# A hybrid decoder block on one core: first attention values from x, and fifteen value products in a new order

## The chip, the cores and the metric

The kernel runs on one core of one Trainium2 chip. Its time is the device time of one execution in microseconds (us); three runs of the kernel before gave 2204.49, 2204.80 and 2205.09 us.

## The reference, cut to what matters

One sequence of 1024 tokens with 1024 channels passes a block of retention and dilated attention, and then an MLP. Only its head matters here:

```python
mod = silu(c) @ w_ada + b_ada            # shift, scale, ... of 1024 channels each
h = rms_norm(x, norm1_g) * (1 + scale) + shift
proj = h @ w_in                          # rq, rk, rv (2048 wide), rg, three groups of aq, ak, av (512 wide each), gates
```

With r(t) the reciprocal root mean square of token t, and a1 = norm1_g (1 + scale), the row of h for token t is r(t) a1 x(t) + shift. So for a weight W, h W = r(t) (a1 x(t)) W + shift W, in which the second part is one row for all tokens.

## The kernel before, in words

Everything is float32. TensorE multiplies in a rounded form (fp32r); each float32 factor is split into a rounded part (`hh`, "hi") and a remainder (`hl`, "lo"), and a product is three matmuls: hi by lo, lo by hi, hi by hi (`mm3`, L203 to L211). ScalarE (ACT) writes the rounded part, VectorE (DVE) the remainder. A matmul of these stages has 128 rows, 128 stationary columns and 512 moving columns.

All instructions stand in an order written out by hand; each engine runs its own in that order, and the DMAs that SP issues are in one order too, which stops where a DMA has to wait for its buffer. Buffers come from pools: `x4` tiles (26 of 512 KB), `wraw` (3, raw weights), `whl` (3 each for `wh` and `wl`). TensorE's results lie in eight banks of PSUM.

The stages, and what they run:

- **Start** (`startup`, L401 to L442). SP loads c, all of x by rows of tokens (`xn`, 8 tiles of 512 KB), the constants, and then for each of 8 row blocks k of 128 channels two rows of the modulation weights (`em`, scale and shift) and the channel-major block of x (`xt`, 512 KB each). ACT squares each `xn` (L428) for the mean square, POOL takes the power (L380), and two sets of four small matmuls (`rstd_bcast`, L387) spread r(t) over the partitions. DVE makes each modulation value by a product with silu(c), 128x1024, with its sum (`mod1`, L463).
- **First attention values** (`av_first`, `av_k`, L796 to L849). For each k, DVE scales `xt` by a1 and r(t) (`h1_scale`, L486), ACT adds the shift and rounds (L488), DVE takes the remainder (L491), and TensorE adds 24 matmuls onto eight banks, one for each block of 128 tokens (L811): group 0.
- **Other attention values** (`av_step`): the same with 192 matmuls each for groups 1 and 2. Beside them, DVE and ACT make sums of blocks of h (`sums_of_h`, t1, t2, t3; L884 to L902; t4 comes in the next stage).
- **Queries, keys, gates** (`queries_keys`, L1007): 18 pairs, each a 2 by 2 block product by seven products of 12 matmuls (Winograd's form: 11, s1, s3, s2, 12, 22, s4 use blocks of h or their sums, and blocks of the weight or their sums). Beside them DRAM to DRAM copies and additions prepare weight sums for later (`copy_block`, `quarter_sums`; the additions are POOL's DMAs that accumulate, L564).
- **Retention values** (`values`, L1117): two halves of seven products of 48 matmuls each, with weights from those sums; `v_post` (L1087) puts the results together, and writes them to `v_d` in DRAM.
- Then retention itself, attention, and the MLP, which the change doesn't touch.

## Time and profile before

| | |
|---|---|
| median of three runs | 2204.8 us |
| profiled execution, first to last instruction (span) | 2203.6 us |
| what the median has beyond that span | 1.2 us |
| TensorE (PE) busy | 2170.7 us, 99% |
| VectorE (DVE), ScalarE (ACT), GpSimd (POOL) busy | 1456.9, 922.9, 160.6 us |

The profile is of one execution, whose time beyond its span isn't listed. A row of a timeline has the start, the duration, the engine, the line, and what is written from what; in brackets stands the idle time before it and what ended that. Matmuls overlap: one takes 0.39 us in a row, while the next begins 0.23 us after it.

### The profile page before, as it was taken

To read this page: it belongs to the slowest core of one execution; us is meant where nothing else is said; L and a number is where in the kernel's file an instruction comes from. 1 tells how busy PE (TensorE), PEld (TensorE's weight loads), DVE (VectorE), ACT (ScalarE), POOL (GpSimd) and SP (SyncE) were. 2 spreads that over 40 slices of the span, in tenths; PEclk is the share of its full clock that TensorE was granted. 3 is DMA by queue.
4 is the path that set the end of the run, shared out by engine and by line. 5 is a ranking of instruction groups with operands and counts; after the bars stand their busy time and mean duration, and the time that the engine had idled before them with its cause. 6 is when DMAs were issued, how large, how long until landed. Compare 5 with 4: busy or idle time off the path is not lost. (4 is left out here: it accounts for less than half of the span.)

```text
span 2203.6 us, 27246 instructions
## 1 busy us (share of the span) xinstructions
PE 2170.7 (99%) x10134; PEld 1802.4 (82%) x10134; DVE 1456.9 (66%) x2284; ACT 922.9 (42%) x1691; POOL 160.6 (7%) x192
## 2 busy tenths in 40 slices
PE   7999999999999999999999999999999999999998
PEld 4888888888887888888888888888778888888887
DVE  6618777763547778865564754677876665887855
ACT  4323332223334445444554634524455445533413
POOL 0001111000011122111100000001100000000003
PEclk9999999999999999999999999999999999999999
DMA  9539999634676556557863265654144344745322
GB/s 367 202 128 284 304 289 292 193 115 172 233 267 209 166 179 220 177 161 197 195 173 97 87 244 186 239 179 160 62 166 152 146 149 177 262 136 175 119 86 77
DMA packets 156611, 408.93 MB, mean 186 GB/s; under 512 B 27446, under 2 KB 55357, under 8 KB 153278
## 3 DMA queue, kind: packets, MB, share of 16 engines
q1 hardware_dynamic: 148542, 363.14, 46.8%
q0 software_dynamic: 7936, 44.05, 9.2%
q8 instruction: 80, 1.31, 0.2%
q14 instruction: 53, 0.43, 0.1%
HBM read 316.27 MB, written 156.13 MB: 214 GB/s over the span
## 5 line engine op out<-in xcount | busy, mean ns | idle before, releaser
L207 PE MATMUL qap<-hh,qaw 128*128 128x512 f32 x216 | 84.0, 389 | 0.0
L209 PE MATMUL qap<-hl,qaw 128*128 128x512 f32 x216 | 84.0, 389 | 0.0
L211 PE MATMUL qap<-hh,qaw 128*128 128x512 f32 x216 | 84.0, 389 | 0.0
L638 POOL TENSOR_TENSOR j<-qk,j 128x512 fp32r<-128x512 f32 x32 | 43.3, 1353 | 458.3 <-ACT j L637 441.7
L1902 POOL TENSOR_TENSOR accnf<-accnf,sqnf 128x256 f32<-128x256 f32 (+1 forms) x18 | 16.6, 922 | 609.6 <-ACT sqnf L1898 609.6
L2006 ACT ACTIVATE a<-a 128x512 f32<-128x512 f32 x48 | 30.3, 631 | 73.3 <-DVE a L2005 73.3
L1322 ACT ACTIVATE P<-P,ng 128x128 f32<-128x128 f32 (+1 forms) x96 | 42.0, 439 | 37.5 <-DVE ng L1319 37.5
L264 DVE TENSOR_TENSOR qaw<-wa,qaw 128x512 fp32r<-128x512 f32 x54 | 36.0, 685 | 30.4 <-ACT qaw L254 30.4
L2214 ACT CAST w2h<-w2s 128x512 fp32r<-128x512 f32 x36 | 22.4, 622 | 80.0 <-DVE w2s L2252 78.8
L264 DVE TENSOR_TENSOR fw<-w1r,fw 128x512 fp32r<-128x512 f32 x48 | 32.9, 688 | 33.6 <-ACT fw L254 33.6
L207 PE MATMUL fp<-h2h,fw 128*128 128x512 f32 x128 | 50.0, 391 | 0.0
L211 PE MATMUL fp<-h2h,fw 128*128 128x512 f32 x128 | 49.8, 389 | 0.0
L209 PE MATMUL fp<-h2l,fw 128*128 128x512 f32 x128 | 49.8, 389 | 0.0
L207 PE MATMUL roa<-rh,rwl 128*128 128x512 f32 x128 | 49.8, 389 | 0.0
L209 PE MATMUL roa<-rl,rwh 128*128 128x512 f32 x128 | 49.8, 389 | 0.0
L211 PE MATMUL roa<-rh,rwh 128*128 128x512 f32 x128 | 49.8, 389 | 0.0
L1737 DVE TENSOR_TENSOR rwl<-rwl,rwh 128x1024 fp32r<-128x1024 f32 x25 | 30.2, 1221 | 29.0 <-ACT rwh L1767 29.0
L673 ACT COPY sm<-sT 128x128 f32<-128x128 f32 x32 | 8.5, 267 | 93.8 <-PE sT L661 93.8
L207 PEld LDWEIGHTS qap<-hh,qaw 128*128 128x128 f32 x216 | 40.6, 188 | 8.5
L211 PEld LDWEIGHTS qap<-hh,qaw 128*128 128x128 f32 x216 | 40.6, 188 | 8.4
L209 PEld LDWEIGHTS qap<-hl,qaw 128*128 128x128 f32 x216 | 40.6, 188 | 8.4
L1902 POOL TENSOR_TENSOR accn<-accn,sqn 128x512 f32<-128x512 f32 x12 | 15.5, 1293 | 392.2 <-ACT sqn L1898 392.2
(3104 smaller groups left out, 7211.6 us busy)
## 6 DMA issues: line engine op xcount, KB each, us to landing
v<-vd SPq DMA_DIRECT2D x32, 512.0 KB, 5.0
raw<-in_w_ada_dram SPq DMA_DIRECT2D x32, 512.0 KB, 5.0
w1r<-in_w_ff_dram SPq DMA_DIRECT2D x32, 512.0 KB, 4.8
vd<-vo SPq DMA_DIRECT2D x24, 512.0 KB, 6.4
yt<-y POOLq DMA_DIRECT2D x24, 512.0 KB, 6.9
xsd<-as SPq DMA_DIRECT2D x24, 512.0 KB, 2.7
w2r<-in_w_ff2s_dram SPq DMA_DIRECT2D x24, 512.0 KB, 7.2
em<-in_w_ada_dram SPq DMA_DIRECT2D x16, 512.0 KB, 10.2
```

The costliest lines, as they stand in the source:

```text
L207: nc.tensor.matmul(o, wl, xh, start=first, stop=False, skip_group_check=skip)
L209: nc.tensor.matmul(o, wh, xl, start=False, stop=False, skip_group_check=skip)
L211: nc.tensor.matmul(o, wh, xh, start=False, stop=last, skip_group_check=skip)
L264: nc.vector.tensor_sub(t[:, 512:], src, fv(t[:, :512]))
L638: nc.gpsimd.tensor_sub(t[:, 1], src, fv(t[:, 0]))
L673: nc.scalar.copy(sm, ps[:, :C])
L1322: nc.scalar.activation(v, v, AF.Exp, bias=ng[:, blk:blk + 1], accum_out=st[:, g, blk, 2 + a:3 + a])
L1737: nc.vector.tensor_sub(lo, fv(lo), fv(hi))
L1902: (nc.vector if f == 7 else nc.gpsimd).tensor_add(G["acc", key], G["acc", key], sq)
L2006: nc.scalar.activation(o, o, AF.Relu)
L2214: nc.scalar.copy(hi, src)
```

## The change

The first attention values (group 0) are made from a1 x without r(t) and without the shift: `plain_split`, `plain_low`; the result is multiplied by r(t) when it leaves PSUM. The shift's row is made beside the later products: DVE multiplies the raw weight's rows by the shift and adds them up in the tile `decay` (`shift_rows`), one float32 matmul with ones adds over the partitions, and four accumulating DMAs add it to the values in DRAM (`shift_out`). So x by rows, r(t), and the modulation's shifts are loaded after the first blocks of weights, and c is loaded straight to 128 partitions. The bias table's and constants' loads are issued from ACT's queue.

Then `more_values` runs eleven products of 48 matmuls. The first four are the retention values' products 11 and 12 of both halves, whose blocks of h and of the weight are not sums (`r0`, `r1`). Block 11 is finished there; the bare product 11 is kept in DRAM (`m11_d`), and `values` copies it back into PSUM (`v_base`). The other seven (`av`) give the attention values of groups 1 and 2 as one 1024 wide product in Winograd's form; its weight sums are made by POOL's accumulating DMAs into SBUF (`u_add`). `values` then has five products for each half in place of seven, and the copies of the weights for the moved ones go. The rows of h are made in halves between these products (`h_scale`, `h_split`), and so are the sums t1 to t4; the last remainder is always queued behind the next step (`late_low`). `a_load(1, ...)`, the table `decay` and cosines are loaded at other places, as the code shows.

```diff
-        xn = [x4(f"xn{b}") for b in range(NC)]
-        for b in range(NC):
-            nc.sync.dma_start(xn[b], io["x"][b])
...
-        for b in range(NC):
-            nc.scalar.activation(xn[b], xn[b], AF.Square, accum_out=ss1[:, b:b + 1])
-        for g in range(3):
-            bias_rows(g)
-        rs = rstd_of(ss1, "n1", xpool)
-        mod1(0)
...
+    def late_low(f=None):
+        if first["lows"]:
+            first["lows"].pop()()
+        if f:
+            first["lows"].append(f)
+    def plain_split(k, ts):
+        nc.scalar.mul(hh[k][:, ts], xt[k][:, ts], a1[:, k:k + 1])
+    def plain_low(k):
+        nc.vector.scalar_tensor_tensor(hl[k], xt[k], a1[:, k:k + 1], fv(hh[k]), op0=ALU.mult, op1=ALU.subtract)
+    def scale_mod(k):
+        mod1(k, (SC1,))
+        nc.vector.scalar_tensor_tensor(a1[:, k:k + 1], mods[:, SC1 + k:SC1 + k + 1], bs1[:, k:k + 1],
+                                       vec[:, VC_N1 + k:VC_N1 + k + 1], op0=ALU.add, op1=ALU.mult)
+    def shift_mod(k):
+        mod1(k, (SH1,))
+        sh = mods[:, SH1 + k:SH1 + k + 1]
+        nc.vector.tensor_add(sh, sh, vec[:, VC_BADA + SH1 + k:VC_BADA + SH1 + k + 1])
+    def h_scale(k, j):
+        t = xt[k][:, 512 * j:512 * j + 512]
+        nc.vector.scalar_tensor_tensor(t, t, a1[:, k:k + 1], rb1[0][:, 512 * j:512 * j + 512],
+                                       op0=ALU.mult, op1=ALU.mult)
+    def h_split(k, j):
+        ts, sh = slice(512 * j, 512 * j + 512), mods[:, SH1 + k:SH1 + k + 1]
+        t, hi, lo = xt[k][:, ts], hh[k][:, ts], hl[k][:, ts]
+        nc.scalar.activation(hi, t, AF.Identity, bias=sh)
+        late_low(lambda: nc.vector.scalar_tensor_tensor(lo, t, sh, fv(hi), op0=ALU.add, op1=ALU.subtract))
...
+              if src != "w_rv" or n not in ("11", "12")]
...
+    def first_values(ahead):
+        H0, H1 = slice(0, 512), slice(512, 1024)
+        nc.sync.dma_start(vec, io["vec"])
+        nc.sync.dma_start(cb, io["c"].to_broadcast([P, D]))
+        nc.scalar.dma_start(rel[:32], io["rel_bias"])
+        for g in range(3):
+            nc.scalar.dma_start(bias_cut(onehot, g)[:33], io["onehot"][:, 384 * g:384 * g + 384])
+        nc.scalar.dma_start(ct, io["cst"])
+        nc.vector.memset(rel[32:33], 1.0)
+        loads = []
+        for k in range(NK):
+            loads += [(xn_load, b) for b in {3: (0, 1, 2), 4: (3, 4), 5: (5,), 6: (6, 7)}.get(k, ())]
+            loads += [(ada_load, SC1 + k), (x_load, k)]
+            if k == 0:
+                loads.append((wa_load, 0, (H0, H1)))
+            if k in (2, 4, 6):
+                loads.append((wa_load, k // 2))
+        loads += [(ada_load, SH1 + k) for k in (0, 2, 4, 6)] + [(u_load, 0)]
+        loads += [(ada_load, SH1 + k) for k in (1, 3, 5, 7)] + [(u_load, 1)]
+        def more(n):
+            for f, *args in [loads.pop(0) for _ in loads[:n]]:
+                f(*args)
+        more(17)
+        nc.scalar.activation(cb, cb, AF.Silu)
+        nc.vector.tensor_scalar_add(bs1, vec[:, VC_BADA + SC1:VC_BADA + SC1 + NK], 1.0)
+        for g in range(3):
+            bias_rows(g)
+        scale_mod(0)
+        wa_split(0, (H0,))
+        plain_split(0, H0)
+        plain_split(0, H1)
+        wa_split(0, (H1,))
+        wh, wl = (fv(t) for t in wa[0][1:])
+        plain_low(0)
+        nc.vector.tensor_sub(wa[0][2][:, H0], wa[0][0][:, H0], wh[:, H0])
+        av = [ps_s(f"av{c}") for c in range(NC)]
+        def mms(k, parts, cs_=range(NC)):
+            w, ws = wa[k // 2][1:], slice((k % 2) * 512, (k % 2) * 512 + 512)
+            for c in cs_:
+                for x, j in parts:
+                    nc.tensor.matmul(av[c], x[k][:, c * C:(c + 1) * C], w[j][:, ws], start=k == 0 and (x, j) == (hh, 0),
+                                     stop=k == NK - 1 and (x, j) == (hl, 0), skip_group_check=True)
+        squares = {2: (0, 1, 2), 3: (3, 4), 4: (5,), 5: (6, 7)}
+        for k in range(NK):
+            more((2, 3, 4, 5, 6, 9, 2, 0)[k])
+            for b in squares.get(k, ()):
+                xn_square(b)
+            if k + 1 < NK:
+                scale_mod(k + 1)
+                for ts in (H0, H1):
+                    plain_split(k + 1, ts)
+                if k % 2 == 1:
+                    wa_split((k + 1) // 2)
+                plain_low(k + 1)
+                if k == 0:
+                    nc.vector.tensor_sub(wa[0][2][:, H1], wa[0][0][:, H1], wh[:, H1])
+                if k % 2 == 1:
+                    raw, hi, lo = wa[(k + 1) // 2]
+                    nc.vector.tensor_sub(lo, raw, fv(hi))
+            if k == 5:
+                rs = rstd_of(ss1, "n1", xpool)
+                rb1.append(x4("rb1"))
+            if k == 0:
+                mms(k, [(hh, 0)])
+                mms(k, [(hl, 0)])
+                mms(k, [(hh, 1)])
+            elif k < NK - 1:
+                mms(k, [(hh, 1), (hh, 0)])
+                mms(k, [(hl, 0)])
+        for m in range(4):
+            shift_mod(2 * m)
+        u_w(0, 0)
+        u_w(0, 1)
+        late_low()
+        for c in range(NC):
+            mms(NK - 1, [(hh, 1), (hh, 0), (hl, 0)], [c])
+            if c % 2 == 0:
+                t = x4(f"avo{c}")
+            o = t[:, DV * (c % 2):DV * (c % 2) + DV]
+            nc.scalar.mul(o, av[c], rs[:, c:c + 1])
+            nc.sync.dma_start(va_d[0][c * C:(c + 1) * C], o)
+            if c in (3, 5):
+                j = (c - 3) // 2
+                nc.scalar.copy(rb1[0][:, 512 * j:512 * j + 512], rstd_bcast(rs, 4 * j, 4, f"n1{j}"))
+            if c == 3:
+                h_scale(0, 0)
+                h_split(0, 0)
+        for m in range(1, 4):
+            h_scale(2 * m, 0)
+            h_split(2 * m, 0)
+        late_low()
+    UPLAN = {"11": ("11", 1, "a"), "12": ("21", 1, "b"), "s1": ("t1", 1, "c"), "s2": ("t2", -1, "a"),
+             "s4": ("22", 1, "c"), "s3": ("t3", -1, "a"), "22": ("t4", -1, "a")}
+    USEQ = [("r0", "11"), ("r1", "11"), ("r0", "12"), ("r1", "12")] + [("av", n) for n in UPLAN]
+    U = {}
+    m11_d = [dram.tile([P, 4, 512], F32, name=f"m11d{hp}") for hp in range(2)]
...
+    def u_load(i):
+        n = USEQ[i][1]
+        for j in range(2):
+            if i in (1, 7):
+                t = x4(f"ur{i}{j}")
+            elif i in (3, 5, 9):
+                t = whl.tile([P, 1024], F32, tag=("wh", "wl")[j], name=f"ur{i}{j}")
+            else:
+                t = wraw.tile([P, 1024], F32, tag="raw", name=f"ur{i}{j}")
+            U["raw", i, j] = t
+            nc.sync.dma_start(t, u_block(i, "21" if n[0] == "s" else n, j))
+    def u_add(i):
+        n = USEQ[i][1]
+        for blk in {"s1": ("22",), "s2": ("22", "11"), "s4": ("11", "12"), "s3": ("11",)}[n]:
+            for j in range(2):
+                if n == "s4":
+                    U["raw", i, j] = U["raw", i - 2, j]
+                nc.gpsimd.dma_start(U["raw", i, j], u_block(i, blk, j), accum_op=ALU.add, max_dma_last_dim=8192)
+    def u_w(i, j):
+        sign, src = float(UPLAN[USEQ[i][1]][1]), U["raw", i, j]
+        hi, lo = u_place(i, "h", j), u_place(i, "l", j)
+        nc.scalar.activation(hi, src, AF.Copy, scale=sign)
+        U["w", i, j] = hi, lo
+        if sign > 0:
+            late_low(lambda: nc.vector.tensor_sub(lo, src, fv(hi)))
+        else:
+            late_low(lambda: nc.vector.scalar_tensor_tensor(lo, src, -1.0, fv(hi), op0=ALU.mult, op1=ALU.subtract))
+    def u_post(i, p):
+        s, n = USEQ[i]
+        if s != "av":
+            ps, hp = U["ps", (s, "a", p)], int(s[1])
+            if n == "11":
+                if p % 2 == 0:
+                    U["m", s] = x4(f"um{s}{p}")
+                t = U["m", s][:, 512 * (p % 2):512 * (p % 2) + 512]
+                nc.scalar.copy(t, ps)
+                nc.sync.dma_start(m11_d[hp][:, p], t)
+                return
+            t = x4(f"uo{s}{p}", F32R).rearrange("p (a b) -> p a b", a=2)
+            nc.scalar.copy(t[:, 0], ps)
+            nc.vector.tensor_sub(t[:, 1], ps, fv(t[:, 0]))
+            nc.sync.dma_start(v_d[2 * hp][:, p], fv(t))
+            return
+        ps = U["ps", (s, UPLAN[n][2], p)]
+        if n == "11":
+            U["r", p] = x4(f"ur{p}")
+        r1, r2 = (U["r", p][:, 512 * j:512 * j + 512] for j in range(2))
+        if n in ("11", "s2"):
+            nc.scalar.copy(r1, ps)
+            return
+        if n == "s1":
+            nc.scalar.mul(r2, ps, -1.0)
+            return
+        if n == "22":
+            nc.scalar.mul(r1, ps, -1.0)
+        elif n == "s3":
+            nc.vector.tensor_sub(r2, r2, ps)
+        else:
+            nc.vector.tensor_add(r1, r1, ps)
+        blk = {"12": "11", "s4": "12", "s3": "22", "22": "21"}[n]
+        c = p + 4 * (int(blk[1]) - 1)
+        nc.sync.dma_start(va_d[int(blk[0])][c * C:(c + 1) * C], r2 if n == "s3" else r1)
+    def shift_rows(k):
+        t, sh = wa[k // 2][0][:, 512 * (k % 2):512 * (k % 2) + 512], mods[:, SH1 + k:SH1 + k + 1]
         if k == 0:
+            nc.vector.tensor_scalar_mul(decay, t, sh)
         else:
+            nc.vector.scalar_tensor_tensor(decay, t, sh, decay, op0=ALU.mult, op1=ALU.add)
+    def shift_out():
+        ps = ps_s("shw")
+        nc.tensor.matmul(ps, ones.to_broadcast([P, P]), decay, start=True, stop=True)
+        t = x4("shw")
+        for j in range(2):
+            nc.scalar.copy(t[:, 512 * j:512 * j + 512], ps)
+        for i in range(4):
+            dst = va_d[0][2 * C * i:2 * C * (i + 1)].rearrange("(a p) x -> p a x", p=P)
+            nc.gpsimd.dma_start(dst, t.rearrange("p (a x) -> p a x", a=2), accum_op=ALU.add)
+    def more_values(ahead):
+        last = len(USEQ) - 1
+        post = []
+        def ready(*fs):
+            for f, *args in fs:
+                f(*args)
+        for i, (s, n) in enumerate(USEQ):
+            if i in (0, 1, 2, 3, 8):
+                u_load(i + 2)
+            for k in {4: (6, 7), 5: (9,), 6: (8,)}.get(i, ()):
+                if k != 8:
+                    u_load(k)
+                u_add(k)
+            if i == 0:
+                for m in range(4):
+                    for p in range(4):
+                        u_mm(0, p, [m])
+                u_w(1, 0)
+                u_w(1, 1)
+                for m in range(4):
+                    shift_mod(2 * m + 1)
+                late_low()
+                for m in range(4):
+                    shift_rows(2 * m)
+                post = [(0, p) for p in range(4)]
+                sh = mods[:, SH1:SH1 + NK].rearrange("p (m j) -> p m j", j=2)
+                nc.vector.tensor_sub(dsh1, sh[:, :, 0], sh[:, :, 1])
+                continue
+            for p in range(4):
+                u_mm(i, p)
+                while post:
+                    u_post(*post.pop(0))
+                post.append((i, p))
+                if i == 1:
+                    h_scale(2 * p + 1, 0)
+                    h_split(2 * p + 1, 0)
+                elif i == 2:
+                    h_scale(2 * p, 1)
+                    shift_rows(2 * p + 1)
+                elif i == 3:
+                    sums_of_h("t1", [p])
+                elif i == 4:
+                    h_scale(2 * p + 1, 1)
+                elif i == 5:
+                    sums_of_h("t2", [p])
+                elif i == 6:
+                    h_split(2 * p + 1, 1)
+                    sums_of_h("t4s", [p])
+                elif i == 7:
+                    h_split(2 * p, 1)
+                    sums_of_h("t3", [p - 1] if 0 < p < 3 else [2, 3] if p else [])
+                elif i == 8:
+                    if p == 0:
+                        for m in range(4):
+                            nc.sync.dma_start(h12_d[m][:, 0], fv(hh[2 * m][:, 512:]))
+                            nc.sync.dma_start(h12_d[m][:, 1], fv(hl[2 * m][:, 512:]))
+                    if p > 0:
+                        sums_of_h("t4", [p - 1])
+                elif i == 9:
+                    if p == 0:
+                        sums_of_h("t4", [3])
+                        nc.sync.dma_start(cs, io["cossin"])
+                    if p == 1:
+                        late_low()
+                        a_load(0, 1)
+                        a_load(0, 2)
+                elif i == last:
+                    BA.prep((0, ORDER[p]))
+                if i < last and p > 1:
+                    u_w(i + 1, p - 2)
+                    if p == 3:
+                        late_low()
+                if i == 2 and p == 3:
+                if i == last and p == 0:
+                    shift_out()
+        BA.flush()
+        u_post(*post.pop())
...
-    VSEQ = [(hp, n) for hp in range(2) for n in VPLAN]
+    VSEQ = [(hp, n) for hp in range(2) for n in VPLAN if n not in ("11", "12")]
...
+    def v_base(hp, p):
+        if p % 2 == 0:
+            V["m", hp] = x4(f"vm{hp}{p}")
+            nc.sync.dma_start(V["m", hp].rearrange("p (a b) -> p a b", a=2), m11_d[hp][:, p:p + 2])
+        V["ps", "a", p] = ps_s(f"va{hp}{p}")
+        nc.scalar.copy(V["ps", "a", p], V["m", hp][:, 512 * (p % 2):512 * (p % 2) + 512])
...
+                if n == "s1" and p > 0:
+                    v_base(hp, p - 1)
+                if n == "s2" and p == 0:
+                    v_base(hp, 3)
...
-    for kk in range(4):
-        steps.add(av_first(kk), [(io["w_av"][kk], split_first)], manual=True)
-    for g in (1, 2):
-        for kk in range(4):
-            steps.add(av_step(g, kk), [(io["w_av"][4 * g + kk], split_first if (g, kk) == (1, 0) else split_w)])
-    steps.mark()
+    steps.add(first_values, manual=True)
+    steps.add(more_values, manual=True)
```

## What is predicted

> **What bounds the kernel now.** I read the page's busy times first, then the waits of TensorE (engine and line, what it waited for: us in total, times, longest).
>
> ```profile
> span 2203.6 us, 27246 instructions
> ...
> PE 2170.7 (99%) x10134; PEld 1802.4 (82%) x10134; DVE 1456.9 (66%) x2284; ACT 922.9 (42%) x1691; POOL 160.6 (7%) x192
> ```
>
> ```profile
> PE n10rb L387 <- POOL n1rs L380: 8.6, 1, 8.6
> PE av L811 <- ACT hh L488: 3.5, 5, 1.2
> ```
>
> TensorE is the bound nearly everywhere; its one long wait is for r(t) at the start. So the change is worth what it takes off TensorE's stream, what it cuts from the start, and minus any new gap. The timeline of TensorE gives the marks between which I count.
>
> ```profile
> 2.46 3.75 PE L425 MATMUL pc<-crow,orow 1*128 1x512 f32 x4 [2.46 <-DMA crow<-in_c_dram]
> 6.87 3.99 PE L447 MATMUL pb<-onehot,rel 33*12 33x384 f32 x6 [0.66 <-DMA onehot<-in_onehot_dram]
> 19.51 2.08 PE L387 MATMUL n10rb<-ct,n1rs 128*128 128x128 f32 x8 [8.65 <-POOL n1rs L380]
> 21.38 1.91 PE L387 MATMUL n11rb<-ct,n1rs 128*128 128x128 f32 x8
> 23.18 1.25 PE L811 MATMUL av<-raw_308h,hh 128*128 128x512 f32 x4
> ```
>
> ```profile
> 159.62 0.39 PE L207 MATMUL qap<-hh,qaw 128*128 128x512 f32 x1
> ```
>
> ```profile
> 502.34 0.39 PE L207 MATMUL va<-vwh,hl 128*128 128x512 f32 x1
> ```
>
> ```profile
> 654.66 0.61 PE L207 MATMUL rg<-hh,raw_4676l 128*128 128x512 f32 x2
> ```
>
> From 502.34 to 654.66 run the 14 x 48 = 672 matmuls of the retention values: 152.32 / 672 = 0.2267 us each, and no gap. The 1512 of the pairs before them (18 x 7 x 12, from 159.62) give the same 0.2267. The first value matmul starts at 23.18; 576 of them should take 130.6, but the pairs start 136.4 later: 5.9 us are gaps, while VectorE is full:
>
> ```profile
> 23.00:75.00 52.00, 48.38 (x205) 37.78 (x204) 43.66 (x63) 17.57 (x23) 0.00 (x0) 1.00 0.75 282
> ```
>
> (Window, length, busy PE, PEld, DVE, ACT, POOL, granted clock, DMA share, GB/s.)
>
> **The change, part by part.**
>
> *Matmuls.* Before: 576 + 672 = 1248. After: 192 + 11 x 48 + 10 x 48 = 1200. Removed: 48 x 0.2267 = **-10.9 us**, on the path, since TensorE had no gap where they stood.
>
> *The start.* The first matmul now needs c, one modulation row, one block of x, half a weight tile, and in ACT's order the three bias copies.
>
> ```profile
> 12.86 1.06 ACT L428 ACTIVATE xn<-xn 128x1024 f32<-128x1024 f32 x1 [0.84 <-DMA xn<-in_x_dram]
> ...
> 17.37 0.46 ACT L449 COPY onehot<-pb 12x384 f32<-12x384 f32 x1
> ```
>
> ```profile
> 10.00:50.00 40.00, 28.30 (x115) 21.38 (x114) 29.67 (x48) 16.62 (x24) 2.57 (x1) 1.00 1.03 408
> ```
>
> The sixth `xn` landed at 12.8 with 3.43 MB ahead of and in it. The half weight tile will have 2.12 MB, 1.31 MB less: at 408 GB/s 3.2 us earlier, 9.6. Cast of half a tile 0.62 and split 0.72 (rows below) make 11.0. The bias matmuls run 6.87 to 10.86; with the last copy (0.46), cast and split that is 12.7, or 11.5 if their loads, first on ACT's queue, come 1.2 earlier. I take 12.0 (bounds 10.5 and 13.5): 12.0 - 23.18 = **-11.2 us**. DVE's first modulation (1.22) is done before.
>
> The Trainium skill ("DMA: Bandwidth & Descriptors", Queues, rings and completion order) says that an engine takes turns between the queue rows that have work, packet by packet: ACT's queue is no path of its own, so the 0.23 MB of bias and constants still delay c and x by an estimated 0.6 us, which the 2.12 MB hold; were it a path of its own the first matmul would be at 11.4 at best. No row of before has two such queues.
>
> *Gaps of the old start*: **-5.9 us**; new ones are counted below.
>
> *New in TensorE's stream.* r(t) was spread ahead of 23.18; now its eight matmuls stand inside block 7: 2 x (21.38 - 19.51) = 3.7. The shift's float32 matmul has 512 columns like the two `pc`, 3.75 for both: 1.9. **+5.6 us**.
>
> *New gaps.* After a block's sources are there, what counts is VectorE and ScalarE between one product and the next.
>
> ```profile
> L463 DVE SCALAR_TENSOR_TENSOR em<-em,cb 128x1024 f32<-128x1024 f32 x16 | 19.3, 1220 | 0.0
> L817 ACT COPY avo<-av 128x512 f32<-128x512 f32 x24 | 13.3, 601 | 33.5 <-PE av L811 31.2 <-DMA vad<-avo 1.3
> L491 DVE SCALAR_TENSOR_TENSOR hl<-xt,mods,hh 128x1024 fp32r<-128x1024 f32 x8 | 10.3, 1284 | 0.6
> ...
> L900 ACT CAST xat<-xt 128x512 fp32r<-128x512 f32 x12 | 7.4, 622 | 10.3 <-DVE xt L884 3.5 <-DVE xt L887 3.4 <-DVE xt L890 3.4
> L898 DVE TENSOR_TENSOR xat<-xt,xat 128x512 fp32r<-128x512 f32 x9 | 6.2, 688 | 0.1
> ...
> L890 DVE SCALAR_TENSOR_TENSOR xt<-xt,mods,xt 128x512 f32<-128x512 f32 x4 | 2.9, 746 | 0.0
> ```
>
> ```profile
> 22.40 0.72 ACT L488 ACTIVATE hh<-xt,mods 128x512 fp32r<-128x512 f32 x1 [0.79 <-DVE xt L486]
> ```
>
> ```profile
> 98.86 0.74 DVE L890 SCALAR_TENSOR_TENSOR xt<-xt,mods,xt 128x512 f32<-128x512 f32 x1
> 99.52 0.68 DVE L898 TENSOR_TENSOR xat<-xt,xat 128x512 fp32r<-128x512 f32 x1
> 100.12 0.75 DVE L890 SCALAR_TENSOR_TENSOR xt<-xt,mods,xt 128x512 f32<-128x512 f32 x1
> ```
>
> Back to back, a half tile costs DVE 0.60 to 0.66, a full tile about 1.2; a result handed over costs its full duration.
>
> Row block 0 has 24 matmuls, 5.4 us. Before block 1 can run, DVE does the remainder of x (1.28), of half the weight (0.6), the next modulation (1.22 + 0.3), waits for ACT's two splits (1.4), and does the next remainder (1.28) and the other half weight (0.6): 6.7, begun about 0.75 after the first matmul: 7.4 against 5.4, **2.0 us** gap. Later blocks need DVE 3.5 to 4.1 and ACT 2.5 to 5.1 against 5.4: none.
>
> In the eleven products, the next weights' low parts are made in the last quarter: after quarter 2 ends (12 x 0.2267 = 2.72 us a quarter), DVE must be done with low half 0 within 2.95, and with half 1 within 4.3. Products by the code:
>
> - 0 and 1: shift modulations and splits, no wait for TensorE's results: DVE is done about 0.3 to 0.7 ahead. 0.
> - 2 (block 11's result): drain 0.3, ACT copy 0.6, DVE 0.69 + 0.66 (`h_scale`) + 0.66 (`shift_rows`) + 1.2 = 4.1: gap 1.2.
> - 3 (also t1): ACT's cast 0.62 and hi half 1.05 stand ahead of the copy, then 0.6, 0.7, 0.6, 1.2: half 0 is 1.5 late, half 1 another 0.7: 2.2.
> - 5 (t2): its result is added by DVE alone: 0.3. 7 (two of t3 in the last quarter, five casts and copies on ACT before the low part): 1.6. 8 (t4's casts on ACT wait until 2 MB of h are saved to DRAM, behind 1 MB of weights on SP's queue): the row below and the queue's order give the first cast at 6 to 9 us of product 8's 10.9; half 1 is then wanted 12.5 after its start, done at 12 to 13: 0. The others: 0.
>
> ```profile
> h12d<-hh SPq DMA_DIRECT2D x4, 256.0 KB, 8.6
> ```
>
> Sum 5.3, with 2.0: **+7.3 us** of gaps; bounds 2 (each engine a little ahead) and 20 (2.2 at eight of ten changes of product, and 2.0).
>
> *Accumulating DMAs.* The s weights come from POOL's DMAs; the longest chain (s4: two in a row from the end of product 5, wanted 16 us later).
>
> ```profile
> wrvs<-in_w_rv_dram POOLq DMA_DIRECT2D x16, 512.0 KB, 8.7
> ```
>
> ```profile
> DMA to landing us min/median/max: 5.2/9.0/18.2
> ```
>
> (The second: all of L564.) At 5.2 two land, with issues, 13.8 after; at 8.7 the second half lands about 21, and some 2 us show. Those rows stand where the DMA engines are full (share 0.95 below); this stage loads 11 MB in 120 us, so I take the nearest, the short end: 0.
>
> ```profile
> 160.00:300.00 140.00, 140.00 (x620) 115.95 (x619) 107.90 (x173) 47.19 (x82) 18.62 (x26) 1.00 0.95 298
> ```
>
> The Trainium skill ("DMA: Bandwidth & Descriptors", Anatomy of one DMA) fits POOL's DMAs at 2.0 us plus bytes over 436 GB/s. By that estimate 512 KB take 3.2, and the term stays 0; the trace's least is 5.2, and the row decides.
>
> *Hidden.* The rest of x's rows and the shifts land while blocks 2 to 7 run: 15 MB at 408 GB/s end by 42, block 7 starts near 51. Squares cost ACT up to 3.7 in one block, with 5.4 there. `v_base`'s eight copies (0.6) and reads stand a product ahead; eight fewer 512 KB copies leave the next stage.
>
> ```profile
> 502.00:655.00 153.00, 153.00 (x677) 126.73 (x676) 72.52 (x90) 59.87 (x84) 7.10 (x10) 1.00 0.65 226
> ```
>
> There DVE and ACT are under half busy. If that cover went, ACT's reads would show at 2 to 3 us a half.
>
> **Sum**: -10.9 - 11.2 - 5.9 + 5.6 + 7.3 = -15.1. The span would be 2188.5; the median of the runs lies 1.2 above the span, so 2204.8 - 15.1 = **2189.7 us**.
>
> **The rivals.**
>
> *A, VectorE becomes the bound in the products.* For it: DVE has 84% of 23 to 75 now, and each quarter brings it 2 to 2.6 of 2.72. Against: moved work is spread over 120 us, in part of which DVE is idle now (0.00 of 20 us here):
>
> ```profile
> 140.00:160.00 20.00, 20.00 (x90) 16.58 (x89) 0.00 (x0) 3.53 (x6) 0.00 (x0) 1.00 0.12 45
> ```
>
> Gaps 12 to 20 in place of 7.3: 2194.4 to 2202.4.
>
> *B, slower than before: late sums.* If each accumulating DMA takes 18.2 us as the longest row, s1 is some 3.5 us late, s2 10 more (two in series, behind s1's on POOL), s4 another 10: +24, 2213. Behind ACT's cast that waits stand the copies that empty PSUM, so TensorE stops at the next product. It passes the old time when the three together are over 15.1 late, at about 15 us a DMA. Against: the 18.2 stands where the engines are full.
>
> *C, the start isn't earlier* (c to 128 partitions or the bias copies hold ACT until r(t) would have been ready): without the 11.2 it is 2200.9.
>
> **How the numbers follow.** Forecast with gaps 2 to 12 and start 10.5 to 13.5: 0.59, 2183 to 2194. A 0.23, B 0.07, C 0.05, unnamed losses 0.03, unnamed gains 0.03. The range from 2183 to 2200 takes the forecast, most of A and leaves the rest. About 0.2% (4.4 us) is what a measurement can tell from none: faster, under 2200.4, is the forecast, most of A and the gains: 0.84; same, up to 2209.2: 0.07; slower 0.09.
>
> **What would show it.** First value matmul near 12; TensorE's next gap about 2 us before block 1, named by DVE; gaps of 1 to 2 us at the starts of products 3 and 4 behind DVE's low parts; 1200 large matmuls; pairs starting near 187, 27 later than now, and 342.7 long; `values` 108.8 long. A start over 14, gaps over 12 in sum, or a wait of TensorE or ACT for an accumulating DMA would make the prediction wrong.

## The result and the profile after

The changed kernel takes 2221.1 us (median of 4 runs, 2219.9 to 2221.9), the kernel before 2204.6 beside it (4 runs, 2204.5 to 2205.1): a ratio of 1.0073, with a 95% interval of 1.0059 to 1.0088. It is slower by 0.7%, where I had forecast 0.7% faster. In the profiled execution the span went from 2203.6 to 2220.1. The page of the changed kernel begins:

```profile
span 2220.1 us, 27323 instructions
...
PE 2170.3 (98%) x10084; PEld 1795.9 (81%) x10084; DVE 1484.3 (67%) x2325; ACT 943.3 (42%) x1730; POOL 175.5 (8%) x208
```

TensorE runs 50 instructions fewer, as it should, yet is busy for the same 2170 us. So matmuls were slower somewhere, and there is 17 us more without any. (A gap in this text is the time between the starts of two matmuls less the usual 0.23; the idle time that a row shows in brackets is 0.2 to 0.6 shorter.) The marks from TensorE's timeline (start, duration, line, tiles) say in which stage:

```profile
11.54 3.78 PE L844 MATMUL av<-wv0wh,hh 128*128 128x512 f32 x8 [1.70 <-ACT hh L410]
15.12 2.41 PE L844 MATMUL av<-wv0wh,hl 128*128 128x512 f32 x8
17.37 2.20 PE L844 MATMUL av<-wv0wl,hh 128*128 128x512 f32 x9
...
59.10 0.40 PE L207 MATMUL ur0a<-uwh,hl 128*128 128x512 f32 x1
...
206.46 0.39 PE L207 MATMUL qap<-hh,qaw 128*128 128x512 f32 x1
...
556.52 0.39 PE L207 MATMUL vc<-vwh,xat 128*128 128x512 f32 x1
...
668.58 0.62 PE L207 MATMUL rg<-hh,raw_4756l 128*128 128x512 f32 x2
```

The first value matmul starts at 11.54 (forecast: 12.0) and the row blocks end at 59.1. From there things go wrong: the pairs start at 206.5 (forecast: 187), last 350.1 (342.7), the values last 112.1 (108.8), and what follows takes 1551.5 (1548.9 before). The eleven products hold most of the loss, some 19 us. The same stage by windows (window, length, busy PE, PEld, DVE, ACT, POOL, granted clock, DMA share, GB/s):

```profile
60.00:130.00 70.00, 66.80 (x285) 52.55 (x283) 52.78 (x77) 30.18 (x45) 2.83 (x3) 1.00 0.70 241
130.00:140.00 10.00, 4.47 (x8) 2.57 (x9) 3.69 (x5) 3.23 (x4) 0.89 (x1) 0.60 1.06 249
140.00:150.00 10.00, 10.00 (x41) 8.15 (x40) 4.52 (x7) 3.92 (x7) 3.52 (x4) 0.89 1.05 243
...
160.00:170.00 10.00, 6.25 (x20) 3.91 (x18) 3.89 (x6) 3.09 (x5) 1.01 (x2) 0.81 0.78 127
170.00:180.00 10.00, 8.26 (x27) 6.28 (x27) 4.25 (x7) 5.90 (x9) 0.00 (x0) 0.68 0.71 270
```

Up to 130 it goes nearly as forecast: 3.2 us without a matmul, at the full clock. Two places are bad, 130 to 140 and 160 to 175, which are the starts of products 6 and 8 (numbered from 0, as in the prediction): TensorE is idle there, and behind each hole the granted clock is down to 0.60 and 0.68. No engine is full: VectorE is busy for 3.7 to 4.5 of 10 us. The waits of TensorE and then of ACT (engine and line, what it waited for: us in total, times, longest) name the chain:

```profile
PE uavc L207 <- ACT uwh L937: 9.4, 3, 4.8
...
PE qap L207 <- DVE qat L293: 3.8, 1, 3.8
...
PE va L207 <- ACT va L1327: 1.5, 1, 1.5
```

```profile
ACT uwh L937 <- DMA ur<-in_w_av_dram: 21.3, 6, 7.1
...
ACT qaw1s L254 <- DMA vad<-shw: 9.7, 1, 9.7
```

ACT can't round the weights of products 6 to 8 because their raw sums, made by POOL's accumulating DMAs, haven't landed. That is the wait that I had named as the sign of a wrong prediction. But it isn't rival B as I had it: one such DMA takes 7.8 us, not 18.2, and B reached the old time only at about 15.

```profile
ur<-in_w_av_dram POOLq DMA_DIRECT2D x12, 512.0 KB, 7.8
```

They began late. POOL's timeline, and ahead of it SP's:

```profile
91.87 0.44 SPq L447 DMA_DIRECT2D browd<-rows  x1
94.37 2.50 SPq L450 DMA_DIRECT2D biasd<-browd  x4
...
107.09 2.39 SPq L450 DMA_DIRECT2D biasd<-browd  x4
109.58 1.01 SPq L922 DMA_DIRECT2D ur<-in_w_av_dram  x2
...
113.63 4.24 SPq L922 DMA_DIRECT2D ur<-in_w_av_dram  x4
```

```profile
124.55 2.03 POOL L931 DMA_DIRECT2D ur<-in_w_av_dram  x2 [78.12 <-DMA ur<-in_w_av_dram]
...
133.66 0.89 POOL L931 DMA_DIRECT2D ur<-in_w_av_dram  x1 [5.77 <-issue]
```

The change also moved the attention bias tables' trip through DRAM to the last quarter of product 2. On SP's in-order queue each of the three tables is a store, a wait until it is in DRAM, and four spreading copies that read it back: from 91.87 to 109.5 SP is taken. The loads of the raw weights of product 5 go out behind that at 109.58, those of 6 and 7 from 113.63, and POOL's first sum at 124.55, five us before product 6 is due. (The kernel before made the same trip from 55.4 to 74.2, on the same queue, and TensorE had no wait over 0.6 us in the 100 us from 60 on.)

**Theory A**, then: SP's order makes the raw weights late. **Theory B**: the sums are too slow wherever their loads stand. **Theory C**: VectorE is the bound in the products, and the waits only name what came last. For the 7.3 us of the queries (from 206.46 to 556.52 less 342.72) there was a fourth, **shw**: the shift row's staging tile is held until the last of four accumulating DMAs has read it, and the next weights wait for that tile (the wait of 9.7 above).

### The profile page after: what moved, and what is told of

The parts are those of the page before. It is cut to its first block, busy times and chain, and to the rows that moved or that the text cites. A ratio compares the mean times of both kernels' runs of the same rounds, so it can differ in the third digit from the quotient of the medians.

```text
span 2220.1 us, 27323 instructions
## 1 busy us (share of the span) xinstructions
PE 2170.3 (98%) x10084; PEld 1795.9 (81%) x10084; DVE 1484.3 (67%) x2325; ACT 943.3 (42%) x1730; POOL 175.5 (8%) x208
## 3 DMA queue, kind: packets, MB, share of 16 engines
q0 software_dynamic: 10752, 52.44, 11.2%
## 5 line engine op out<-in xcount | busy, mean ns | idle before, releaser
L2218 ACT ACTIVATE a<-a 128x512 f32<-128x512 f32 x48 | 30.3, 632 | 73.6 <-DVE a L2217 73.6
L2219 ACT ACTIVATE a<-a 128x512 f32<-128x512 f32 x64 | 40.5, 633 | 2.0
```

The costliest lines, as they stand in the source:

```text
L2218: nc.scalar.activation(o, o, AF.Relu)
L2219: nc.scalar.activation(o, o, AF.Square)
```

## The experiments

Each ran beside the kernel before on the same chip. The ratio is to it, with its 95% interval.

**1. The bias tables on POOL's queue, at row block 0.**

```
-        nc.sync.dma_start(brow_d[g], ...)      # and the four spreading copies
+        nc.gpsimd.dma_start(brow_d[g], ...)
-                if i == 2 and p == 3:          # call moved to row block 0
```

> The 15 DMAs of the bias tables (three to DRAM, twelve that spread them) leave SP's order between products 2 and 3 and are issued by POOL beside row block 0. Theory A (SP's order holds the raw weights of products 5 to 8, and with them the sums): the loads for products 6 and 7 are issued 10 us or more earlier, the waits before products 6 and 8 go, 2204 to 2210 us. Theory B (each accumulating DMA is too slow even when its load is on time): 2215 to 2221. Theory C (VectorE is the bound in the products): no change from 2221.

Measured: 2215.4, ratio 1.0048 (1.0031 to 1.0065). Product 6 has no gap any more. But product 0 started at 63.3 instead of 59.1, since the tables now share full DMA engines (share 1.03) with the row blocks' loads: gaps of 1.0 and 1.5 behind weights, and 0.8 ahead of r(t). The products, from 59.1 to 206.5 (147.4) before, take 133.9. That speaks for A, but the total does not: 2215.4 lies in B's range, since 4.2 us went at the start and product 8 keeps gaps of 2.5 and 2.5, which theory A expected to go.

**2. The shift row a product earlier.**

```
-                if i == last and p == 0:
+                if i == 9 and p == 0:
                     shift_out()
```

> The shift's row (one matmul, two copies, four accumulating DMAs of POOL) is made in product 9 in place of product 10. If its tile, which stays taken until the last of its four DMAs has read it, is what stops ScalarE and then TensorE in pair 1 of the queries, the 5 us of gaps there and their slow matmuls go: 2213 to 2217. If the late loads of pair 1 are the cause: 2219 to 2222. Theories A, B and C on the products say nothing of it.

Measured: 2218.1, ratio 1.0057 (1.0042 to 1.0072). The pairs take 348.6 instead of 350.1, and the gap of 4 stays: POOL's four DMAs go out from 187.9 to 211.3 now, not from 200.0 to 226.2, and that isn't early enough. It decides nothing about the theory.

**3. No accumulating DMAs for the raw weights.** All twelve are left out, so the weights of products 6 to 9 aren't sums here.

```
-                nc.gpsimd.dma_start(U["raw", i, j], u_block(i, blk, j), accum_op=ALU.add, ...)
```

> The twelve accumulating DMAs that make the attention values' weight sums are left out (the weights of s1, s2, s3, s4 are then plain blocks). What they cost in all, whether by their own length (B) or by what is late ahead of them (A): without them the waits before products 6, 7 and 8 go under A and B, 2202 to 2209. Theory C: 2218 to 2221. If it ends well above e1, the loads alone are late enough to hold TensorE.

Measured: 2206.6, ratio 1.0004 (0.9995 to 1.0013). Products: 130.2. The sums and the wait for them are worth 17 us in the products, and VectorE does all that it did, so theory C is out. Products 6 and 8 still start with two gaps of about 1 each. The queries' gaps (1.8 and 4.0) are unchanged, and the wait behind them too (waits of ACT):

```profile
ACT qaw1s L254 <- DMA vad<-shw: 9.9, 1, 9.9
```

**4. Experiments 1 and 2 together.**

> e1 and e2 together. Theory A and the tile's wait: 2197 to 2203, below the kernel before. Theory B: 2207 to 2215.

Measured: 2210.5, ratio 1.0027 (1.0016 to 1.0038). Products 134.1, pairs 347.8; a gap of 3.3 at 38.6 among the row blocks is the price of the tables there. With it the total is again in B's range, and A's number (2197 to 2203) is missed. So the tables have to go neither on SP at product 2 nor beside the row blocks.

**5. The tables on POOL, from product 0 on.** A copy of the rows onto themselves on ACT holds them until then.

```
+        nc.scalar.copy(bias_cut(rows, g)[:12], bias_cut(rows, g)[:12])
+        nc.gpsimd.dma_start(brow_d[g], ...)
```

> The changed kernel with the 15 DMAs of the bias tables on POOL's queue, let go only once ACT has touched their rows at product 0 (near 60 us), away from SP's order and away from the row blocks of the start. Theory A (SP's order is what makes the raw weights of products 5 to 8 late): product 4 starts at 105 as in the changed kernel, product 6 has no gap over 1.2, the pairs start near 193 (197.2 less the 4.2 that the tables cost at the start in the run before), about 2211. Theory B (each accumulating DMA is too slow whenever it is issued): the gap of 5 before product 6 stays and the pairs start at 205 or later, about 2220.

Measured: 2207.4, ratio 1.0011 (1.0001 to 1.0020), better than A's own number. The tables pass between 65 and 88 and no new gap shows there. POOL's first sum starts 14.7 us earlier (POOL's timeline), and product 6 starts without a gap (TensorE's):

```profile
109.87 0.97 POOL L932 DMA_DIRECT2D ur<-in_w_av_dram  x1 [21.93 <-DMA ur<-in_w_av_dram]
```

```profile
127.54 0.40 PE L207 MATMUL uavc<-uwh,xat 128*128 128x512 f32 x1
...
152.10 0.50 PE L207 MATMUL uavc<-uwh,hl 128*128 128x512 f32 x1 [2.34 <-ACT uwh L938]
153.37 0.50 PE L209 MATMUL uavc<-uwl,hh 128*128 128x512 f32 x1 [0.76 <-DVE uwl L941]
```

The pairs start at 191.8, 14.7 us earlier: that much of the some 19 us is SP's order. (That is one execution of ten, which lie between 2204.2 and 2210.9; by the medians the kernel gained 13.7.) The sums themselves are no faster than before (their median is 8.2), so B as a matter of one DMA's duration is out for products 6 and 7. What remains is product 8, whose sums are two DMAs in a row a tile.

**6. The shift row at product 3, its four DMAs at product 7**, on top of 5.

```
+                if i == 3 and p == 0:
+                    shift_out()          # matmul and copies into the staging tile
+                if i == 7 and p == 0:
+                    shift_add()          # the four accumulating DMAs
```

> The kernel before this one, and the shift row worked out at product 3, with its four accumulating DMAs issued at the head of product 7 instead of the last product. Theory shw (the queries' gaps come from the staging tile that these four DMAs hold until the last has read it): the gap of about 4 in the first pair is gone, the pairs take 343 to 345 instead of 350, about 2204. Rival (the queries' gaps come from VectorE's own work in the first pair): gap and 350 stay, about 2211. Second rival: at product 7 these four DMAs make the sums of product 8 later, and the gap there grows by up to 4 transfers of 3.8.

Measured: 2226.8, ratio 1.0101 (1.0086 to 1.0116). Both sides of theory shw can be read here. The pairs take 342.7 (219.9 to 562.6), the ideal, without any gap: the queries' gaps were the staging tile's. And that tile, now held from 97 to 179, does the same to product 8, on a larger scale:

```profile
180.72 0.80 PE L207 MATMUL uavc<-uwh,hl 128*128 128x512 f32 x1 [28.45 <-ACT uwh L938]
```

```profile
ACT xat L1133 <- DMA vad<-shw: 31.0, 1, 31.0
```

The first row is from TensorE's timeline, the second from ACT's waits: the cast that stands ahead of product 8's weights on ACT needs the tile that the shift's DMAs read until 179. My rival was four transfers of 3.8 (15 us); it was 28.6, because a tile is only free when the last transfer has landed and POOL issued them 6.4 apart, behind product 8's own sums.

**7. The values' base loaded a product earlier**, on top of 6.

```
+            if q == NA - 1 and n == "11":
+                v_base_load(0)
+            if (hp, n) == (0, "22"):
+                v_base_load(1)
```

> The kernel before this one, and the loads of the values' base (two of 512 KB a half) issued a product earlier. If the gap of 1.7 to 3.2 at the first product of the values is ACT waiting for these loads, it is gone and the values take 109 to 110 instead of 112 to 114, about 2201. If it is ACT's own work there, the values stay at 112 and the time at that of the kernel before this one.

Measured: 2222.2, ratio 1.0078 (1.0062 to 1.0095), 4.6 under experiment 6. The values take 109.7 instead of 113.1 and their first gap is gone. In experiment 6 the wait there was (waits of ACT between 560 and 600):

```profile
ACT va L1333 <- DMA vm<-m11d: 4.2, 1, 4.2
```

**8. Holds in the kernel before.** At seven places of the pairs 14 to 17, the next product's weights wait for a chain of POOL additions.

```
+            for _ in range(HOLD[q, n]):          # 1, 2, 3, 4, 5, 7, 9
+                nc.gpsimd.tensor_add(hold, hold, hold)
+            nc.gpsimd.tensor_add(w, fv(w), hold[:, :1])
```

> The kernel before the change, with TensorE held between products at seven places of the pairs 14 to 17, by one, two, three, four, five, seven and nine POOL additions that the next product's weights wait for. If an idle TensorE alone lowers the granted clock, the short gaps (about 1 to 2 us) leave the matmuls at 0.227 us and the long ones (over some 3 us) bring 0.43 us for the 4 to 8 us behind them, as in the changed kernel at 134 and 166 us. If the slow matmuls there came from the transfers beside them, all seven places stay at 0.227 us.

Measured: 2282.2 (one run). The holds came out longer than meant, 4.6 to 8.4 us, so the short end wasn't tried here. Behind every one of the seven the matmuls come 0.43 apart at first; the last but one in TensorE's timeline, and a window behind it, in which the DMA engines moved nothing:

```profile
527.20 0.80 PE L210 MATMUL qap<-hh,qaw 128*128 128x512 f32 x1 [8.26 <-POOL qaw L1035]
527.79 0.63 PE L212 MATMUL qap<-hl,qaw 128*128 128x512 f32 x1
528.22 0.63 PE L214 MATMUL qap<-hh,qaw 128*128 128x512 f32 x1
...
530.35 0.63 PE L212 MATMUL qap<-hl,qaw 128*128 128x512 f32 x1
530.78 0.46 PE L214 MATMUL qap<-hh,qaw 128*128 128x512 f32 x1
```

```profile
527.00:530.00 3.00, 2.80 (x7) 2.22 (x8) 0.00 (x0) 0.00 (x0) 0.14 (x1) 0.50 0.00 0
```

The clock is 0.50 for 3.6 us, with a DMA share of 0.00. In three of the seven holds the DMA engines moved nothing in the hold either, and the pace behind was the same. So the idle time lowers the clock, not the transfers beside it. Each of the seven holds cost about 1.5 to 2.8 us on top of its own length. The rest of the added time lies in and behind the holds and isn't used here.

**9. A staging tile of its own for the shift row**, at its old place, on top of 5, and with 7.

```
-        t = x4("shw")
+        shw = xpool.tile([P, 512], F32, tag="shw", bufs=1, name="shwt")
```

> The kernel with the bias tables on POOL from product 0 on, the shift row at its old place in the last product but staged in a tile of its own (eight accumulating DMAs of 256 KB from 512 columns, none of the shared tiles held), and the values' base loaded a product earlier. Theory shw (the queries wait for the shared staging tile): the pairs take 343 instead of 349, the values 110 instead of 112, about 2198. Rival (the queries' gaps come from VectorE, or from a shared tile that something else holds): the pairs stay at 348 or more, about 2204.

Measured: 2195.7, ratio 0.9955 (0.9937 to 0.9973). Pairs 342.7, values 108.8: both ideal. This is theory shw without the harm of experiment 6, since nobody else asks for that tile. (The eight smaller transfers also went out within 13 us, where the four had taken 26; what each of the two is worth was not separated.)

**10. Product 8's sums ahead of product 9's on POOL**, on top of 9.

```
-            for k in {4: (6, 7), 5: (9,), 6: (8,)}.get(i, ()):
-                if k != 8:
-                    u_load(k)
-                u_add(k)
+            for k in {4: (6, 7), 5: (9,)}.get(i, ()):
+                u_load(k)
+            for k in {4: (6, 7), 6: (8, 9)}.get(i, ()):
+                u_add(k)
```

> The kernel before this one with the sums of product 8 issued before those of product 9 on POOL. Theory (product 8's gaps of 2.5 + 1.0 + 2.5 + 1.0, and the slow matmuls behind them, come from its two accumulating DMAs a tile, one after the other and late in POOL's order): its first accumulating DMA goes near 131 instead of 136.5, about 5 of the 8 us go, about 2193. Rival (the rate of these DMAs, one in 3.8 us, is the limit): product 9 is late instead, and the time stays near 2198.

Measured: 2189.2, ratio 0.9923 (0.9906 to 0.9941). It beats both kernels. Product 8's gaps are 1.2 and 1.0, instead of 2.7, 1.0, 2.5 and 1.0; product 9 isn't late. Its page and its marks:

```profile
span 2187.7 us, 27339 instructions
...
PE 2159.6 (99%) x10084; PEld 1793.6 (82%) x10084; DVE 1484.1 (68%) x2325; ACT 944.2 (43%) x1732; POOL 185.8 (8%) x227
```

```profile
187.11 0.39 PE L207 MATMUL qap<-hh,qaw 128*128 128x512 f32 x1
...
529.83 0.39 PE L207 MATMUL vc<-vwh,xat 128*128 128x512 f32 x1
...
638.62 0.62 PE L207 MATMUL rg<-hh,raw_4762l 128*128 128x512 f32 x2
```

With the same 10084 instructions TensorE is busy 10.7 us less than in the changed kernel: most of that is the slow matmuls.

**11. Product 7's loads and sums a product earlier**, on top of 10.

```
-            for k in {4: (6, 7), 5: (9,)}.get(i, ()):
+            for k in {3: (7,), 4: (6,), 5: (9,)}.get(i, ()):
                 u_load(k)
-            for k in {4: (6, 7), 6: (8, 9)}.get(i, ()):
+            for k in {3: (7,), 4: (6,), 6: (8, 9)}.get(i, ()):
                 u_add(k)
```

> The kernel before this one with the loads and sums of product 7 a product earlier, at the head of product 3. If POOL's order still holds product 8, its gaps are now 1 or less and the time about 2191. If the tile that product 8 shares with product 6 decides (its sums can't begin before product 6's weights are split, near 130), nothing is gained. Against it: the four transfers of product 7 are now in front of those of product 6, and a gap of 1 to 4 can come before product 6, about 2195.

Measured: 2192.2, ratio 0.9940 (0.9924 to 0.9955), 3.0 over experiment 10. Product 8's gaps stay (1.2 and 1.0), and neither of my two readings fits: from experiment 10 on, ACT waits for no sum there. Its cast of the second half of these weights stands behind two casts of t3, which wait for VectorE (ACT's timeline in experiment 10):

```profile
149.06 0.62 ACT L1127 CAST xat<-xt 128x512 fp32r<-128x512 f32 x1 [0.76 <-DVE xt L1114]
150.51 0.62 ACT L1127 CAST xat<-xt 128x512 fp32r<-128x512 f32 x1 [0.83 <-DVE xt L1114]
151.04 1.05 ACT L938 ACTIVATE uwh<-ur 128x1024 fp32r<-128x1024 f32 x1
```

That is the gap that the prediction had for product 7 (two of t3 in the last quarter, 1.6), and no order of the sums removes it. The sums of 6, now behind those of 7, are late by a little (TensorE's timeline):

```profile
130.97 0.50 PE L207 MATMUL uavc<-uwh,xat 128*128 128x512 f32 x1 [0.90 <-ACT uwh L938]
```

That is the case against it, at its lower end.

## Why the prediction was wrong

The stages side by side, in us, from the first starts in TensorE's timeline. "Products" is from product 0's start to that of the pairs; "rest" is from the retention's first matmul to the end of the span. (The forecast's mark for the pairs, 187, was 1 under what its own sum of 2188.5 implies.)

| kernel | first value matmul | product 0 | products | pairs | values | rest | span |
|---|---|---|---|---|---|---|---|
| forecast | 12.0 | | (pairs at 187) | 342.7 | 108.8 | 1548.9 | 2188.5 |
| changed | 11.5 | 59.1 | 147.4 | 350.1 | 112.1 | 1551.5 | 2220.1 |
| 5, tables at product 0 | 11.2 | 58.6 | 133.2 | 349.1 | 112.5 | 1549.1 | 2202.5 |
| 9, own tile, base early | 11.0 | 58.3 | 133.6 | 342.7 | 108.8 | 1549.8 | 2193.3 |
| 10, product 8 first | 11.1 | 58.5 | 128.6 | 342.7 | 108.8 | 1549.1 | 2187.7 |

- **Matmuls, -10.9: right.** With the gaps gone the values take 108.8 and the pairs 342.7, which is 0.2267 for each matmul that was counted.
- **Start, -11.2: right as a mark, but 2.2 of it is lost at once.** The first value matmul starts at 11.54 for 12.0. In the timeline above row block 0 takes 7.6 us for 24 matmuls, 2.2 too many, without a gap: the first ten come 0.43 apart (eight in 3.58 us), the later ones 0.23, and the trace's record of the full granted clock begins at 15.97 (for a window ahead of that the profile prints 1.00, since nothing is on record). In the kernel before, the record begins at 23.34, so r(t)'s matmuls, which then stood ahead, had been the ones at half pace. The prediction had no term for this.
- **r(t) and the shift, +5.6: 2.9 too high.** From 11.54 to 59.10 are 47.6 us; 192 matmuls take 43.5 and the slow first ten 2.2 more, so 1.8 is left for r(t), where I had put 3.7. The shift's matmul took 0.9 for 1.9 (it and one of 0.23 run from 197.40 to 198.48). My prices came from rows at the slow pace of the start: eight of r(t)'s matmuls took 2.08 us there, and 1.05 here, in the middle of the stream:

```profile
54.54 1.05 PE L383 MATMUL n10rb<-ct,n1rs 128*128 128x128 f32 x8
```

- **New gaps of VectorE and ACT, +7.3: the 2.0 didn't come, the 5.3 did.** Before row block 1 TensorE has no gap at all, where I forecast 2.0 behind VectorE. That 2.2 is lost there all the same is luck: it is the slow pace of the first ten matmuls. Starts of products 3 and 4:

```profile
93.98 0.50 PE L209 MATMUL ur1a<-uwl,hh 128*128 128x512 f32 x1 [0.96 <-DVE uwl L940]
106.08 0.50 PE L209 MATMUL uava<-uwl,hh 128*128 128x512 f32 x1 [0.93 <-DVE uwl L940]
```

  1.1 each with the issue time, named by VectorE's low parts, for 1.2 and 2.2. Product 5 has 1.0 that I had at nothing; that is SP's order too (its load goes out at 109.58), and it is gone in experiment 5. In experiment 10, where no sum is late, the gaps before products 1, 3, 4 and 8 are 0.4, 1.1, 1.0 and 2.2, in sum some 4.8 for my 5.3.
- **Accumulating DMAs, 0: the step that failed.** It read "this stage loads 11 MB in 120 us, so I take the nearest, the short end: 0", and counted the longest chain "from the end of product 5". I asked how long a sum takes, and not when its load can start. The bias tables' stores, waits and copies were part of the change, and they stand on SP ahead of the loads of products 5 to 7; I never followed what they were moved past. That is 14.7 us (experiment 5). The duration was wrong as well, 7.8 in the median for 5.2, and so was the reason for the short end: with its stores, sums and tables the stage moved 33 MB, where I had counted 11 MB of loads, and while the sums ran the DMA engines were full (share 1.02):

```profile
124.00:162.00 38.00, 31.19 (x119) 23.51 (x118) 20.28 (x27) 14.02 (x21) 10.10 (x12) 0.87 1.02 246
```

  So the row of 8.7, where they are full too, was the nearest. With product 9's sums queued ahead of product 8's this cost another 5.0 (experiment 10 against 9).
- **What I never costed: the staging tile of the shift row, 7.3.** I followed the shift's matmul and not its four DMAs. They hold a tile of the shared ring until the last has landed, and the weights of the first pair wait for it (experiments 6 and 9).
- **Hidden `v_base`, 0: wrong by 3.3.** I named a price of 2 to 3 us a half, and engines under half busy as the cover. The loads ran into a wait of ACT at the first product of the values; issued a product earlier they left 0.9 in experiment 7 and nothing in 9.
- **The rest, 2.4**, is a longer wait for the retention's first keys in the changed kernel. It is gone in experiment 5, but no run took it by itself, so its cause is open.
- **The idle TensorE's price.** Every hole of over about 3 us also cost 1 to 3 us of slow matmuls behind it, which no rival of mine had. The hole before product 6 and the clock behind it:

```profile
134.60 0.80 PE L207 MATMUL uavc<-uwh,xat 128*128 128x512 f32 x1 [4.81 <-ACT uwh L937]
135.86 0.79 PE L209 MATMUL uavc<-uwl,xat 128*128 128x512 f32 x1 [0.47 <-DVE uwl L940]
136.45 0.63 PE L211 MATMUL uavc<-uwh,xat 128*128 128x512 f32 x1
136.88 0.63 PE L207 MATMUL uavc<-uwh,xat 128*128 128x512 f32 x1
```

The sum of the misses from the changed kernel to experiment 10: products 147.4 - 128.6 and 0.6 at product 0's start, 19.4; pairs 7.3; values 3.3; rest 2.4: 32.4, which is 2220.1 - 2187.7. Experiment 10 keeps every step of the change that I had costed and takes away what I had not: it stands at 2189.2, where the forecast was 2189.7. That they agree to half a us is luck. Its row blocks and products take 12.8 us more than their 720 matmuls, and I had 12.9 (5.6 and 7.3), but of other parts: 2.6 for r(t) and the shift, 4.8 of gaps, 1.7 for the slow first matmuls, 1.6 for matmuls at half pace behind product 8's gaps, and 2.1 in small pieces. Rival B had the right place (late sums) and the right sign, with a price of 2213; its mechanism, 18.2 us a DMA, was not the one.

## What to carry to other kernels

When a step is moved, write down every DMA it issues and the queue it stands on, and ask of the next load on that queue when it can go out: three small tables with a wait in the middle took an in-order queue for 18 us and cost 15, and on another queue, from product 0 on, they cost nothing (experiment 5). A tile that a DMA reads is busy until that DMA lands; if several slow DMAs read it, give it a tile that nobody else waits for. And cost a gap of TensorE that is longer than about 3 us at 1 to 3 us more than its length.

## What the runs showed of the hardware

- **The clock behind a gap.** After gaps of 3.5 to 8.4 us the matmuls of 512 columns come 0.43 apart instead of 0.227 at once, for 3.1 to 5.7 us (experiment 8; in the changed kernel longer, where more gaps fell into it). After single gaps of 1.0 to 1.6 us they did not. In between it varies: in experiment 5 a gap of 2.5 and one of 1.0 a matmul later were followed by four matmuls at full pace and then by matmuls at half pace from 154.4; in experiment 10 gaps of 1.2 and 1.0 so close were followed by slow matmuls 2.3 us later, and in experiment 3 the like were not. A single gap of 2.1 was followed by slow matmuls (experiment 5, at 221 us), and one of 2.3 in the same kernel wasn't (at 231). The Trainium skill ("TensorE: Matmul & The Clock Gate", What's actually happening) says that the clock falls to half after an idle window of some 3.4 us and is given back after a busy one as long. The half agrees, and 3.1 to 5.7 us is near that length or above it; the pairs of short gaps show that less than one whole idle stretch of 3.4 can be enough.
- **The first matmuls.** In the changed kernel the first ten of the row blocks came 0.43 apart without a gap, and the trace's record of the full clock begins with the next (15.97). In the kernel before, it begins at 23.34, behind r(t)'s matmuls.
- **Accumulating DMAs.** 512 KB from DRAM added into a tile took 7.8 us in the median in the changed kernel, where POOL issued the twelve within 37 us, about one in 3.4, and 8.2 in experiment 5. The four that added the shift row into DRAM went out 6.3 to 12.9 apart.
